# A two-layer diffusion backbone: where the context's low parts stand, and which products carry the modulation sums

## The chip, the cores and the metric

The kernel runs on one core of one Trainium2 chip. The metric is device time in microseconds (us) of one execution, as the median of the runs shown. One execution was recorded by the hardware profiler; its rows give the engines as PE (TensorE's matmuls), PEld (its weight loads), DVE (VectorE), ACT (ScalarE), POOL (GpSimd) and SP (SyncE, which here only issues DMAs). Rows are "start, duration, engine, line, operation, out<-in, shape, count", and in brackets the idle time before the row and what ended it.

## The reference

Two consecutive layers act on 512 latent tokens and 256 context tokens of width 1024. A conditioning vector per kind of token (c for the latents, c_ctx for the context) gives six modulation vectors per layer. Layer 0 mixes tokens with latent attention and neighbourhood attention, layer 1 with a sliding window; each then has a SwiGLU network (width 2816). Cut to what matters here:

```python
for l in range(DEPTH):                       # 2 layers
    sh_a, sc_a, g_a, sh_f, sc_f, g_f = split(silu(c) @ mod_w[l] + mod_b[l], 6)
    csh_a, csc_a, ...                = split(silu(c_ctx) @ mod_w[l] + mod_b[l], 6)
    a_lat = rms_norm(h_lat) * (1 + sc_a) + sh_a
    a_ctx = rms_norm(h_ctx) * (1 + csc_a) + csh_a
    o_lat, o_ctx = mixer(a_lat, a_ctx, ...)          # both kinds use the same weights
    h_lat = h_lat + g_a * o_lat
    h_lat = h_lat + g_f * swiglu(modulate(h_lat, sh_f, sc_f), w_gate_up[l], w_down[l])
    if l == 0: the same for h_ctx with the context's vectors
return rms_norm(h_lat, final_norm)
```

All is float32, and the kernel keeps that accuracy.

## The kernel before

**Products.** TensorE multiplies a rounded format (fp32r) here. Every float32 operand is split into a high part (the rounded value, ACT) and a low part (the rest, DVE), and a product is three matmuls: high by high, high by low, low by high. Splits of weights read L335 (ACT, high) and L336 (DVE, low), and in the pairs below L1377 and L1378. Tokens lie in the columns: 0 to 511 latents, 512 to 767 context; 1024 features are eight tiles of 128 rows.

**Start.** `modulate` (L426) makes the modulated tile k in three steps: a scaled tile (DVE, L433), its high part (ACT, L434) and its low part (DVE, L435). `latent(k)` does so for the 512 latent columns and `context(k)` for the 256 context columns, each followed by products of the kind of L767 to L769 (`three`), which add over k into six PSUM banks, t = 0 to 3 for the latents and 4, 5 for the context. When a latent bank is complete, 128x128 blocks of it are copied out (L502 on DVE, L503 on ACT). Behind this comes the input projection (L346 to L349), whose weights are split by L335 and L336, and further modulation sums of layer 0 (L240 on DVE, L257 on POOL, L258 on ACT).

**Network of layer 0.** The 22 tiles of the hidden width are done in six groups: 0 to 3, 4 to 7, 8 to 11, 12 to 15, 16 to 19, and 20, 21; they are called groups 1 to 6 here. A tile is a `Pair`: gate and up products by a scheme of seven products instead of eight, over two halves of the 768 columns (c1 and c2, 384 each). `head`, `body` and `tail` share it out: the tail of a pair comes behind the head of the next, and the tail of a group's last pair comes just ahead of the group's down products. A pair's weights (two of 512 KB, SP) are combined on DVE (L1412, L1413, L1416, L1420) and split (L1377, L1378). Its tail ends with `t + y` (L1447) and, for c2 and then c1, the product silu x up (L1449), its high part on ACT and its low part on DVE (L1378). After each group but the last come eight down products, m = 0 to 7 (`down0`): the 768-column sum so far ("home") is fetched from memory by POOL (L1233 `p<-home`), the product runs over the group's tiles (L346 to L349) into one bank of 512 and one of 256 columns, DVE adds each to the fetched tile (`add_residual`, L1229), and POOL stores it (L1544 `home<-p`).

**Modulation sums of layer 1.** They need 64 weighted sums over 512 KB blocks of `mod_w`: one DVE instruction each (L302, 128x1024, 1.22 us). 48 blocks are fetched by POOL (L292), all into one buffer (tag `rope0`), 16 of them serve two sums. `late_step(place)` takes the next block: its L302 is placed behind the instruction `place` on DVE, and then the fetch of the following block is issued on POOL. LATE says where the steps are taken: its second part gives for each tile j the number of steps in its pair (the first behind the body, one more behind the preceding pair's tail if the number is over 1, one more behind its own head if over 2); its third part gives for each group the down products m after which a step is taken. When the units have run out, further steps do nothing.

**Order of the work.** A scheduler orders the instructions of each engine by simulated times (SCHED); `behind` and `after` add order constraints between instructions, which need no semaphore on one engine. Each engine then runs its list in order, so an instruction that waits holds up all behind it. POOL's DMA issues are in such a list too.

## Time and profile before

| what | value |
|---|---|
| median of 3 runs | 1574.36 us (1573.1 to 1575.22) |
| profiled execution | 1578.6 us, its span 1576.8 us |
| granted TensorE clock, mean | 0.993 |
| busy in the span | PE 97%, DVE 75%, ACT 50%, POOL 18% |
| chain that ended last | PE 77%, DVE 10%, DMA 6%, ACT 3% |
| L302 (sums of layer 1) | 64 of 1221 ns |
| L292 (their fetches) | 48 of 512 KB |

How to read it: since PE is busy for nearly the whole span, a row of another engine matters where a PE row has brackets that name it, and in what it makes late further on. In a row of the waits by group stand the total, the number and the longest of the waits. In a table by stretch the columns are the stretch, its length, the busy time of PE, PEld, DVE, ACT and POOL with their instruction counts, the granted clock (1.00 is full), the DMA share and GB/s.

### The profile page before, as it was taken

How to read it: one execution, taken by the hardware profiler on the slowest of the kernel's cores; microseconds unless marked ns; L12 is line 12 of the kernel's file. 1: busy time of each engine (PE TensorE's matmuls, PEld its weight loads, DVE VectorE, ACT ScalarE, POOL GpSimd, SP SyncE). 2: the span in 40 equal slices, each digit the busy share in tenths (PEclk: the TensorE clock that was granted, in tenths of full speed). 3: DMA queues.
4: the chain of work that ended last, by engine and by line, in shares of the span. 5: the costliest groups of instructions: out<-in, count | busy, mean ns of one | idle time of the engine just before them, and what ended most of it. 6: DMA issues, size and time to landing. Idle time of an engine off the chain costs nothing.

```text
span 1576.8 us, 26525 instructions
## 1 busy us (share of the span) xinstructions
PE 1529.3 (97%) x10016; PEld 1372.7 (87%) x10016; DVE 1174.8 (75%) x2346; ACT 796.1 (50%) x1607; POOL 276.3 (18%) x302
## 2 busy tenths in 40 slices
PE   6999999999999999999999999999999999999998
PEld 4787778887998999999998988877889999899998
DVE  3885777685878587686858676879976778678685
ACT  4563677775465243242423335558856545354453
POOL 0144724320111101102111132470012000000001
PEclk9999999999999999999999999999999999999999
DMA  9645242004654444647466485110225133323322
GB/s 318 249 131 174 79 127 76 11 7 160 207 168 144 151 167 162 219 126 272 157 198 229 144 325 185 54 41 2 69 76 164 54 97 125 99 89 128 84 97 88
DMA packets 76463, 214.90 MB, mean 136 GB/s; under 512 B 9872, under 2 KB 16400, under 8 KB 76336
## 3 DMA queue, kind: packets, MB, share of 16 engines
q1 hardware_dynamic: 59216, 144.42, 28.1%
q0 software_dynamic: 15968, 67.24, 12.3%
q8 instruction: 78, 1.28, 0.3%
q10 hardware_dynamic: 1152, 1.57, 0.3%
q14 instruction: 49, 0.40, 0.1%
HBM read 186.97 MB, written 23.07 MB: 133 GB/s over the span
## 4 chain that ended last, share of the span: by engine, by line
PE 77%; DVE 10%; DMA 6%; ACT 3%; issue 2%; POOL 0%; SPq 0%; DVEq 0%; ACTq 0%; POOLq 0%
PE pso L557 5%; PE pss L1392 5%; PE pss L1391 5%; PE pss L1390 4%; PE psd L346 4%; PE psd L349 4%; PE psd L348 4%; PE pss L346 4%; PE pss L349 4%; PE pss L348 3%; PE pst L1392 3%; PE pst L1390 3%; PE pst L1391 3%; PE pst L346 3%; PE pst L348 3%; PE pst L349 3%
## 5 line engine op out<-in xcount | busy, mean ns | idle before, releaser
L335 ACT CAST wh<-wr 128x1024 fp32r<-128x1024 f32 (+2 forms) x148 | 115.5, 795 | 208.2 <-DMA wr<-in_w_dn_dram 48.9
L336 DVE TENSOR_TENSOR wl<-wr,wh 128x1024 fp32r<-128x1024 f32 (+2 forms) x145 | 133.0, 924 | 81.1 <-ACT wh L335 79.5
L563 ACT ACTIVATE p<-p,sm 128x512 f32<-128x512 f32 (+3 forms) x144 | 104.9, 729 | 28.5 <-DVE sm L567 26.7
L1390 PE MATMUL pss<-b,wh 128*128 128x384 f32 (+1 forms) x346 | 108.0, 313 | 0.6 <-ACT b L372 0.6
L1391 PE MATMUL pss<-b,wh 128*128 128x384 f32 (+1 forms) x346 | 108.2, 313 | 0.1
L1392 PE MATMUL pss<-b,wl 128*128 128x384 f32 (+1 forms) x346 | 107.3, 312 | 0.0
L348 PE MATMUL psd<-b,wh 128*128 128x512 f32 (+3 forms) x262 | 89.6, 342 | 0.0
L302 DVE CUSTOM_DVE_ANT_0 p<-rope,cond 128x1024 bf16<-128x1024 f32 x64 | 76.9, 1221 | 11.3 <-DMA rope<-in_mod_w_dram 11.2
L292 POOL DMA_DIRECT2D rope<-in_mod_w_dram x48 | 25.7, 535 | 321.1 <-DVE mod L302 308.7
L346 PE MATMUL psd<-b,wh 128*128 128x512 f32 (+3 forms) x222 | 80.0, 361 | 0.9 <-ACT b L476 0.6
L557 PE MATMUL pso<-ph,b 128*64 128x256 f32 (+1 forms) x384 | 78.9, 365 | 0.4 <-DVE ph L502 0.4
L349 PE MATMUL psd<-b,wl 128*128 128x512 f32 (+3 forms) x222 | 78.7, 355 | 0.0
L557 PE MATMUL pso<-pl,b 128*64 128x256 f32 (+1 forms) x384 | 78.5, 363 | 0.0
L1390 PE MATMUL pst<-b,wh 128*128 128x384 f32 (+1 forms) x226 | 70.7, 313 | 2.5 <-DVE p L1229 1.9
L1392 PE MATMUL pst<-b,wl 128*128 128x384 f32 (+1 forms) x226 | 70.7, 313 | 1.4 <-DVE wl L1378 1.4
L1391 PE MATMUL pst<-b,wh 128*128 128x384 f32 (+1 forms) x226 | 70.5, 312 | 0.0
L1377 ACT CAST wh<-pl 128x512 fp32r<-128x512 f32 x78 | 44.9, 620 | 50.0 <-PE pss L1391 22.6
L348 PE MATMUL pss<-b,wh 128*128 128x256 f32 (+3 forms) x216 | 69.2, 321 | 0.0
L1377 ACT CAST wh<-wr 128x1024 fp32r<-128x1024 f32 x39 | 41.0, 1051 | 54.5 <-PE pst L1391 14.6
L346 PE MATMUL pss<-st,wh 128*128 128x512 f32 (+2 forms) x198 | 67.1, 339 | 0.3 <-ACT wh L335 0.3
L349 PE MATMUL pss<-st,wl 128*128 128x512 f32 (+2 forms) x198 | 67.2, 339 | 0.1
L1390 PEld LDWEIGHTS pss<-b,wh 128*128 128x128 f32 x346 | 65.9, 191 | 1.1 <-ACT b L372 0.9
(627 smaller groups left out, 5377.6 us busy)
## 6 DMA issues: line engine op xcount, KB each, us to landing
wr<-in_w_gu_dram SPq DMA_DIRECT2D x88, 512.0 KB, 4.1
rope<-in_mod_w_dram POOLq DMA_DIRECT2D x48, 512.0 KB, 3.9
wr<-in_w_dn_dram SPq DMA_DIRECT2D x73, 256.0 KB, 3.0
wr<-in_w_out_dram SPq DMA_DIRECT2D x32, 512.0 KB, 4.0
p<-home POOLq DMA_DIRECT2D x40, 384.0 KB, 5.4
home<-p POOLq DMA_DIRECT2D x40, 384.0 KB, 5.4
wr<-in_w_in_dram SPq DMA_DIRECT2D x21, 512.0 KB, 4.4
nb<-in_nb_dram SPq DMA_DIRECT2D x16, 384.0 KB, 3.2
```

The source lines that it names most:

```text
L302: behind(V.tensor_tensor_reduce(out=T("p", [P, D], mybir.dt.bfloat16), in0=w, in1=cond[:, v, :], op0=ALU.mult, op1=ALU.add, scale=1.0, sca ...
L335: behind(S.copy(h, r), *after[:1])
L336: behind((G if eng else V).tensor_tensor(lo, r, f(h), op=ALU.subtract), *after[1:])
L346: ins = PE.matmul(o, wh[:, k], mh[:, c], start=first and k == 0, stop=False)
L348: PE.matmul(o, wh[:, k], ml[:, c], start=False, stop=False)
L349: PE.matmul(o, wl[:, k], mh[:, c], start=False, stop=last and k == n - 1)
L557: ins = PE.matmul(o[64 * i : 64 * i + 64, c], v(kt), t, start=n == 0, stop=n == len(moving[i]) - 1)
L563: S.activation(p[:, c], p[:, c], AF.Exp, bias=nm, scale=-1.0, accum_out=dn)
L1377: S.copy(h, t)
L1390: PE.matmul(o, wh, xh, start=first and k == 0, stop=False, skip_group_check=not first)
L1391: PE.matmul(o, wh, xl, start=False, stop=False, skip_group_check=not first)
L1392: PE.matmul(o, wl, xh, start=False, stop=k == 3, skip_group_check=not first)
```

## The change

Two edits. The first changes the table LATE: in groups 3, 4 and 5 the down products take two steps (after m = 2 and 5) where they took four (after 0, 2, 4, 6), and the pairs take more: group 3 one more (8 in all), groups 4 and 5 two more each (10 in all, three in each of the last three pairs), and tiles 20 and 21 take the step that is left over (one sum). The second gives `context(k)` an order constraint: the scaled tile k is placed behind the low part of tile k − 2 on DVE. Lines from 873 on stand two lower in the changed file.

```diff
-LATE = ((0, 1, 3, 5, 7), ()), (0,) * 4 + (1, 2, 2, 2, 1, 2, 2, 2, 1, 2, 3, 2, 1, 2, 3, 2, 0, 0), ((2,), (2,)) + ((0, 2, 4, 6),) * 3
+LATE = ((0, 1, 3, 5, 7), ()), (0,) * 4 + (1, 2, 2, 2, 1, 2, 3, 2, 1, 3, 3, 3, 1, 3, 3, 3, 2, 1), ((2,), (2,), (2, 5), (2, 5), (2, 5))
@@
+    lows = []
+
     def context(k):
-        modulate(A[k], X[k], k, r, 0, 0, 1, CTXS)
+        lows.append(modulate(A[k], X[k], k, r, 0, 0, 1, CTXS, after=lows[-2:-1]))
         for t in (4, 5):
             start_products(k, t)
```

No engine gets more work: PE has 9115 rows in either order, DVE 2332, POOL 299. What moves, at three places.

**DVE at the start**, from the first scaled context tile on. Before (p_564, p_574, ... are the scaled tiles of k = 0, 1, ...; b_99, b_101, ... the low parts):

```order
L433 SCALAR_TENSOR_TENSOR p_564<-b_67,mod_44_123,nb_97 128x256
L433 SCALAR_TENSOR_TENSOR p_574<-b_68,mod_44_123,nb_97 128x256
L433 SCALAR_TENSOR_TENSOR p_584<-b_69,mod_44_123,nb_97 128x256
L433 SCALAR_TENSOR_TENSOR p_594<-b_70,mod_44_123,nb_97 128x256
L433 SCALAR_TENSOR_TENSOR p_604<-b_71,mod_44_123,nb_97 128x256
L433 SCALAR_TENSOR_TENSOR p_614<-b_72,mod_44_123,nb_97 128x256
L433 SCALAR_TENSOR_TENSOR p_624<-b_73,mod_44_123,nb_97 128x256
L433 SCALAR_TENSOR_TENSOR p_634<-b_74,mod_44_123,nb_97 128x256
L502 COPY b_648<-pss_114 128x128
L435 SCALAR_TENSOR_TENSOR b_99<-p_564,mod_42_121,b_98 128x256
L502 COPY b_649<-pss_115 128x128
```

And in the changed kernel:

```order
L433 SCALAR_TENSOR_TENSOR p_564<-b_67,mod_44_123,nb_97 128x256
L433 SCALAR_TENSOR_TENSOR p_574<-b_68,mod_44_123,nb_97 128x256
L502 COPY b_648<-pss_114 128x128
L435 SCALAR_TENSOR_TENSOR b_99<-p_564,mod_42_121,b_98 128x256
L433 SCALAR_TENSOR_TENSOR p_584<-b_69,mod_44_123,nb_97 128x256
L502 COPY b_649<-pss_115 128x128
L502 COPY b_648<-pss_116 128x128
L502 COPY b_649<-pss_116 128x128
L435 SCALAR_TENSOR_TENSOR b_101<-p_574,mod_42_121,b_100 128x256
L433 SCALAR_TENSOR_TENSOR p_594<-b_70,mod_44_123,nb_97 128x256
L502 COPY b_650<-pss_114 128x128
L502 COPY b_650<-pss_115 128x128
```

The low part of tile 0 stands behind two scaled tiles instead of eight, and from there scaled tiles and low parts alternate. Further down in the new order the split of the first projection weight (wl_695) stands between the low parts of tiles 2 and 3.

**DVE at the end of group 4's pairs** (the tail of tile 15) and the first residuals of its down products. Before:

```order
L336 TENSOR_TENSOR wl_8420<-wr_8417,wh_8419 128x512
L1449 TENSOR_TENSOR p_8190<-p_8190,p_8191 128x384
L1447 TENSOR_TENSOR p_8191<-pss_8257,p_8191 128x384
L1378 TENSOR_TENSOR b_8157<-p_8190,b_8156 128x384
L1449 TENSOR_TENSOR p_8190<-p_8190,p_8191 128x384
L1378 TENSOR_TENSOR b_8157<-p_8190,b_8156 128x384
L1229 SCALAR_TENSOR_TENSOR p_8340<-pst_8343,mod_1111_5169,p_8340 128x256
L302 ISA p_8372,mod_1682_8371<-rope_1675_8300,cond_66 128x1024
L302 ISA mod_1682_8371 128x1
L1229 SCALAR_TENSOR_TENSOR p_8340<-psd_8342,mod_1110_5168,p_8340 128x512
```

And in the changed kernel (L1451, L1449, L1380 and L1231 are L1449, L1447, L1378 and L1229 of before):

```order
L336 TENSOR_TENSOR wl_8420<-wr_8417,wh_8419 128x512
L1451 TENSOR_TENSOR p_8190<-p_8190,p_8191 128x384
L302 ISA p_8303,mod_1676_8302<-rope_1674_8260,cond_66 128x1024
L302 ISA mod_1676_8302 128x1
L1449 TENSOR_TENSOR p_8191<-pss_8262,p_8191 128x384
L1380 TENSOR_TENSOR b_8157<-p_8190,b_8156 128x384
L1451 TENSOR_TENSOR p_8190<-p_8190,p_8191 128x384
L1380 TENSOR_TENSOR b_8157<-p_8190,b_8156 128x384
L1231 SCALAR_TENSOR_TENSOR p_8345<-pst_8348,mod_1111_5169,p_8345 128x256
L1231 SCALAR_TENSOR_TENSOR p_8376<-psd_8379,mod_1111_5169,p_8376 128x256
L1231 SCALAR_TENSOR_TENSOR p_8413<-pst_8416,mod_1111_5169,p_8413 128x256
L1231 SCALAR_TENSOR_TENSOR p_8345<-psd_8347,mod_1110_5168,p_8345 128x512
```

A sum now stands between the first L1449 and L1447 of the tail; the one behind the first residual is gone, and the 256-wide parts of residuals 0, 1 and 2 come ahead of the 512-wide ones. At the end of group 5 the rows move in the same way.

**POOL in group 4's down products**, from the load of residual 1 on (home_4258 to home_4265 are the tiles m = 0 to 7). Before:

```order
L1233 DMA p_8376<-home_4259 128x768
L1233 DMA p_8413<-home_4260 128x768
L292 DMA rope_1684_8374<-in_mod_w_dram 128x1024
L1544 DMA home_4258<-p_8340 128x768
L1544 DMA home_4259<-p_8376 128x768
L1233 DMA p_8454<-home_4261 128x768
L1233 DMA p_8491<-home_4262 128x768
L1544 DMA home_4260<-p_8413 128x768
L292 DMA rope_1698_8452<-in_mod_w_dram 128x1024
L1544 DMA home_4261<-p_8454 128x768
L1544 DMA home_4262<-p_8491 128x768
```

And in the changed kernel:

```order
L1235 DMA p_8376<-home_4259 128x768
L1235 DMA p_8413<-home_4260 128x768
L292 DMA rope_1678_8305<-in_mod_w_dram 128x1024
L1546 DMA home_4258<-p_8345 128x768
L1235 DMA p_8454<-home_4261 128x768
L1235 DMA p_8491<-home_4262 128x768
L1235 DMA p_8528<-home_4263 128x768
L1546 DMA home_4259<-p_8376 128x768
L1546 DMA home_4260<-p_8413 128x768
L292 DMA rope_1698_8452<-in_mod_w_dram 128x1024
L1546 DMA home_4261<-p_8454 128x768
L1546 DMA home_4262<-p_8491 128x768
```

The loads of tiles 3, 4 and 5 come directly behind the store of tile 0, where tiles 3 and 4 came behind the store of tile 1 and tile 5 much later.

## The prediction

> **What bounds the kernel now.** I read the page's first part, then the waits of TensorE, then timelines at the places where the change acts.
>
> ```profile
> PE 1529.3 (97%) x10016; PEld 1372.7 (87%) x10016; DVE 1174.8 (75%) x2346; ACT 796.1 (50%) x1607; POOL 276.3 (18%) x302
> ...
> PE pst L810 <- DVE p L387: 12.5, 1, 12.5
> ...
> PE psd L769 <- DVE b L435: 1.2, 1, 1.2
> ```
>
> TensorE works for 1529.3 of 1576.8 us, so all other engines together cost 47.5 us, 12.5 of it one wait at the start that the change doesn't touch. No matmul is removed or added. Only two things can move the time: TensorE's waits, and the speed at which it is clocked. The short wait above, of 1.2, lies at the first place that the diff edits; those at the second are quoted there. I don't gain from DVE's 75%: its work is the same before and after, and only its order counts.
>
> **Part 1, the context's low parts.** The rows are of DVE and TensorE just after the start's latent products.
>
> ```profile
> 53.67 3.26 DVE L433 SCALAR_TENSOR_TENSOR p<-b,mod,nb 128x256 f32<-128x256 f32 x8 [2.48 <-ACT nb L820]
> 56.84 0.29 DVE L502 COPY b<-pss 128x128 f32<-128x128 f32 x1
> 57.04 0.48 DVE L435 SCALAR_TENSOR_TENSOR b<-p,mod,b 128x256 fp32r<-128x256 f32 x1
> ...
> 54.19 0.51 ACT L434 ACTIVATE b<-p,mod 128x256 fp32r<-128x256 f32 x1 [0.55 <-DVE p L433]
> ...
> 56.02 0.39 PE L768 MATMUL psd<-wh,b 128*128 128x512 f32 x1
> ...
> 57.57 0.50 PE L769 MATMUL psd<-wh,b 128*128 128x512 f32 x1 [1.16 <-DVE b L435]
> ...
> 62.32 1.23 DVE L336 TENSOR_TENSOR wl<-wr,wh 128x1024 fp32r<-128x1024 f32 x1 [0.43 <-ACT wh L335]
> ...
> L211 PE MATMUL psd<-ph,cond_col x8: 379/379/403, 116.1 to 116.8; 128*32 128x256 f32 x8
> ```
>
> Before, eight scaled tiles run in a row (3.26 / 8 = 0.41 each), so the first low part comes at 57.04, though its high part is there at 54.19 + 0.51 = 54.70. L769 needs it and waits 1.16. After, two scaled tiles, one copy and low 0: 53.67 + 2 x 0.41 = 54.49, copy to 54.85 (its bank is filled by then, since ACT's copy of a neighbour ran in the same time), low 0 done by 55.3. L769 would start 0.23 behind 56.02, at 56.25. **The wait of 1.16 goes.** Next in line, by the same prices: low 1 needs scaled 2, three copies (0.2 each) and itself, so it is ready at 56.8 against a need at 57.6; low 2 at 58.2 against 59.0. Then the new order lets DVE split the first projection weight (L336, 1.23 long) ahead of low 3: done by 60.2. TensorE covers this with 20-odd products of that projection, which now stand between context tiles 2 and 3 and need the split at about 60.9. If that cover went, the price is at most 1.2 (one L336 before low 3). So part 1 is **−1.2**, bounds −1.2 and +1.2. The background sums of layer 0, which stand behind it on DVE and ACT, begin about 3 us later, because ACT's table load now follows the last high part; the buffers that they hold (ph, pl) are next needed by the products at 116.1 (the last row), and 50 us of TensorE's own projection work lie between, which cover it: nothing, at most 3 if they don't.
>
> **Part 2, fewer sums in the down products.** In group 4 (tiles 12 to 15) TensorE lost most:
>
> ```profile
> 842.53 0.34 PE L1392 MATMUL pss<-b,wl 128*128 128x384 f32 x1
> ...
> 844.74 0.41 PE L1390 MATMUL pst<-b,wh 128*128 128x384 f32 x1 [1.87 <-DVE p L1229]
> ...
> 838.43 0.44 PE L1390 MATMUL psd<-b,wh 128*128 128x384 f32 x1 [0.69 <-DVE p L1229]
> ...
> 828.16 0.75 DVE L1229 SCALAR_TENSOR_TENSOR p<-pss,mod,p 128x512 f32<-128x512 f32 x1 [3.80 <-DMA p<-home]
> ...
> 841.43 0.69 DVE L1412 TENSOR_TENSOR pl<-wr 128x512 f32<-128x512 f32 x1 [2.07 <-DMA wr<-in_w_gu_dram]
> ...
> 843.85 0.75 DVE L1229 SCALAR_TENSOR_TENSOR p<-pst,mod,p 128x512 f32<-128x512 f32 x1
> ...
> 819.77 0.56 POOL L1544 DMA_DIRECT2D home<-p  x1 [4.29 <-DVE mod L302]
> 820.32 1.08 POOL L1233 DMA_DIRECT2D p<-home  x2
> ```
>
> Read from below: POOL issues in order, and what ended the 4.29 us in which it issued nothing was a sum (L302). Only then does it send for the residual tiles 3 and 4 (820.32). They are late, DVE's L1229 waits 3.80 for one, and everything behind it on DVE slips: the next pair's preparation (L1412) gets in front of residual 6, waits 2.07 for its own weights, and TensorE waits 1.87 for that residual's bank. In the new order the loads of residual tiles 3, 4 and 5 follow the store of residual 0 at once, about 4.8 us earlier (POOL was free for them at 819.77 − 4.29 = 815.48 and sent at 820.32), no sum stands between the first three residuals, and both remaining residuals, 6 and 7, precede the second pair's L1412. I take **0.69 + 1.87 = 2.56 off**. The transfers of this stage crowd each other:
>
> ```profile
> 756.00:813.00 57.00, 57.00 (x333) 55.75 (x332) 40.86 (x72) 21.69 (x42) 6.40 (x12) 1.00 0.47 151
> ...
> 813.00:843.00 30.00, 29.18 (x164) 25.79 (x162) 20.22 (x34) 8.38 (x14) 7.01 (x13) 1.00 0.83 288
> ...
> rope<-in_mod_w_dram POOLq DMA_DIRECT2D x8, 512.0 KB, 3.8
> ...
> rope<-in_mod_w_dram POOLq DMA_DIRECT2D x3, 512.0 KB, 7.2
> ...
> wr<-in_w_gu_dram SPq DMA_DIRECT2D x5, 512.0 KB, 7.3
> ```
>
> (First the pairs, then the down products: DMA share 0.47 and 0.83; a sum's 512 KB lands in 3.8 and in 7.2 us.) Two fewer 512 KB fetches there help the rest too, which I don't count.
>
> The stall has a second price, the clock. After 844.74 the matmuls are spaced wider:
>
> ```profile
> 840.00:860.00 20.00, 18.13 (x96) 17.81 (x95) 15.75 (x27) 7.00 (x13) 2.71 (x5) 0.91 0.52 190
> ...
> 845.34 0.34 PE L1391 MATMUL pss<-b,wh 128*128 128x384 f32 x1
> ...
> 848.98 0.34 PE L1392 MATMUL pss<-b,wl 128*128 128x384 f32 x1
> ...
> 851.93 0.33 PE L1392 MATMUL pss<-b,wl 128*128 128x384 f32 x1
> ...
> 213.48 0.63 PE L511 MATMUL psd<-ident_r,p 128*128 128x128 f32 x4 [1.54 <-DVE b L977]
> ```
>
> The window's granted clock is 0.91. From 845.34 to 848.98 lie 12 steps of one matmul in 3.64 us; at the usual 0.174 (848.98 to 851.93 is 17 steps) they would take 2.08. That is 1.56 lost, and it goes with the stall: **−1.56**. A stall of 1.54 at 213.48 is followed by wider spacing as well, those of 0.7 to 1.2 shown here are not.
>
> [...]
>
> Group 5 (tiles 16 to 19) has the same sums, and a smaller stall:
>
> ```profile
> 939.47 1.22 DVE L302 CUSTOM_DVE_ANT_0 p<-rope,cond 128x1024 bf16<-128x1024 f32 x1
> ...
> 940.61 1.22 DVE L1378 TENSOR_TENSOR wl<-wr,wh 128x1024 fp32r<-128x1024 f32 x1
> ...
> 941.88 0.45 PE L1392 MATMUL pst<-b,wl 128*128 128x384 f32 x1 [0.83 <-DVE wl L1378]
> ```
>
> The L302 at 939.47 (1.22) stands just ahead of the split that TensorE waits for. It moves to the pairs: **−0.83**, bounds −0.83 and 0. Group 3 showed no such wait; nothing there.
>
> **What the pairs pay.** Groups 4 and 5 now have three sums in each of their last three pairs. There is one buffer for the sums' weights: a sum, the issue behind it, the landing, the next sum.
>
> ```profile
> 798.42 1.23 DVE L302 CUSTOM_DVE_ANT_0 p<-rope,cond 128x1024 bf16<-128x1024 f32 x1 [0.65 <-DMA rope<-in_mod_w_dram]
> ...
> 799.95 0.53 POOL L292 DMA_DIRECT2D rope<-in_mod_w_dram  x1 [4.84 <-DVE mod L302]
> ...
> 804.26 1.22 DVE L302 CUSTOM_DVE_ANT_0 p<-rope,cond 128x1024 bf16<-128x1024 f32 x1 [1.26 <-DMA rope<-in_mod_w_dram]
> ...
> 807.50 0.55 DVE L1449 TENSOR_TENSOR p<-p,p 128x384 f32<-128x384 f32 x1
> ...
> 809.43 0.55 DVE L1449 TENSOR_TENSOR p<-p,p 128x384 f32<-128x384 f32 x1
> ...
> 810.56 0.56 DVE L1378 TENSOR_TENSOR b<-p,b 128x384 fp32r<-128x384 f32 x1 [0.58 <-ACT b L1377]
> ...
> 811.68 0.28 PE L346 MATMUL pst<-b,wh 128*128 128x256 f32 x1
> ...
> 813.22 0.40 PE L348 MATMUL psd<-b,wh 128*128 128x512 f32 x1
> ```
>
> Both L302 waited for data, so their distance, 804.26 − 798.42 = 5.84 us, is the cycle; the third sum of the last pair can start at 804.26 + 5.84 = 810.1 and ends at 811.3. In the new order it stands between the first L1449 (807.50) and L1447, and DVE can do nothing else meanwhile. Behind it: L1447, the low part of the first half (done near 812.4, where TensorE wants it at about 811.7), L1449, ACT's high part (the wait of 0.58 before 810.56) and the low part of the second half, near 813.9 to 814.1, where the 512-wide products first want it at about 813.2 (L348 multiplies by the low part). So TensorE waits about **0.9 in group 4 and 0.9 in group 5**. Bounds for each: 0 if the sums shift earlier (the cycle without waits is nearer 5.3), and 2.5, two L302 of 1.22 with no margin left. I take 0.9, since the cycle was measured at the same spot. The pairs before have no such tail: their products are followed by the next pair's, which hide 1.22 us of DVE at 75% load. The one sum that ends up in group 6 stands between two products of running pairs: nothing, at most its own 1.22.
>
> **The sum** against the profiled execution (1578.6, span 1576.8, and 1.8 around it): −1.2 − 2.56 − 1.56 − 0.83 + 1.8 = −4.3. The profiled run is 4.2 over the median of the three runs, 1574.36; the difference carried over gives **1570.1**.
>
> **Rivals.**
> A. *The crowd stays.* The weights of the next pair (7.3 to land) delay L1412, not the sums; POOL's earlier loads then only move the crowd forward. For it: the 2.07 was ended by a weight DMA. Against: residuals 6 and 7 now stand ahead of that wait. The group 4 and 5 gains (4.95) fail and the tails cost: 1574.36 − 1.2 + 1.8 = **1575.0**. Chance 0.22.
> B. *The one buffer becomes the bound* (slower). The last fetch of groups 4 and 5 now travels with the loads of residuals 0 to 2 and the first down weights. At the crowded landing of 7.2 instead of 804.26 − 799.95 = 4.31 the third sum starts 2.9 later, TensorE waits 0.9 + 2.9 = 3.8 twice, and both stalls are past 1.54, so the clock drops: 2 x (3.8 + 1.56) = 10.7. 1574.36 − 1.2 − 4.95 + 10.7 = **1578.9**. It decides from waits of about 3 us each, where the gains are eaten. Against: the share before 813 is 0.47. Chance 0.14.
> C. *Part 1 does not pay*: the split of the projection weight takes the place of the wait it removes. 1570.1 + 1.2 = **1571.3**. Chance 0.10.
> D. *The clock drop isn't the stall's* and comes all the same, whatever the waits: 1570.1 + 1.56 = **1571.7**. Against: both drops shown began behind a stall of 1.5 or more. Chance 0.06. [...]
>
> **How the numbers follow.** Forecast 0.48, rivals 0.22, 0.14, 0.10, 0.06. About 0.2% (3.1 us) is what a measurement of this kernel can tell from no change: 1571.2 to 1577.5. The forecast is faster, C straddles the edge (0.02 faster, 0.08 same), A and D are same, B slower: 0.50, 0.36, 0.14. The low end leaves out the tails' cost and takes a little of the run spread: 1570.1 − 1.8 − 0.8 = 1567.5; the high end is A with the same: 1575.8. Forecast alone: 1567.5 to 1572.
>
> **What would show it.** Right: no wait at the first L769; no L1390 of group 4 waiting on L1229, a granted clock of 1.00 there; POOL's loads of residuals 3 to 5 right behind the store of residual 0; waits under 1.5 us on L1449's low parts at the end of groups 4 and 5. Wrong: idle TensorE of 3 us or more at those two tails with L302 waiting for its weights in front (B), or L1229 still late behind L1412 (A).

## The result, and the profile after

| what | before | after |
|---|---|---|
| median of 22 runs each, us | 1575.23 (1573.08 to 1579.12) | 1580.36 (1574.77 to 1585.33) |
| ratio, with its 95% interval | 1 | 1.0029 [1.0020, 1.0037] |
| profiled execution, its span, us | 1578.6, 1576.8 | 1581.22, 1579.5 |

The change makes the kernel slower, by 0.0029 x 1575.23 = 4.6 us. The forecast was 1570.1 and faster; the range ended at 1575.8. First the engines' busy times of the changed kernel, then TensorE's waits by group (total, number, longest); only the rows that are new are shown.

```profile
PE 1529.7 (97%) x10016; PEld 1371.3 (87%) x10016; DVE 1175.2 (74%) x2346; ACT 797.6 (50%) x1607; POOL 274.3 (17%) x302
```

```profile
PE psd L767 <- DVE b L502: 2.6, 1, 2.6
PE psd L1392 <- ACT wh L1379: 1.8, 1, 1.8
...
PE psd L346 <- DVE st L744: 1.0, 1, 1.0
...
PE pst L346 <- DVE st L744: 0.8, 1, 0.8
```

No engine works more than before. The group that part 1 of the prediction aimed at (L769 waiting on L435, 1.2) and those of part 2 (L1390 waiting on L1229) are gone. Four others stand in their place: two at the first input projection (L346 on L744), one between groups 5 and 6 (L1392 on L1379), and one of 2.6 in layer 0's value projection.

**Where the profiled execution is ahead or behind.** The table takes the start of the same-numbered matmul of TensorE in both traces (the changed one minus the other).

| place (time in before) | after minus before, us |
|---|---|
| ahead of the context's products, 50 | −0.5 |
| behind the context's products, 82 | −2.0 |
| behind the first projection, 117 | +0.3 |
| 211, behind a clock drop of before alone (183.4) | −2.2 |
| 270 | +0.2 |
| within group 4's down products, 820 | +1.7 |
| end of group 4, 863 | −1.6 |
| late in group 5's down products, 933 | −1.3 |
| group 6, 973 | +1.0 |
| 1008 | +2.1 |
| end | +2.6 |

Both edits win where they were meant to win (−1.5 from 50 to 82, and −3.3 from 820 to 863) and lose it again a little later. The loss of 2.4 between 211 and 270 is the value projection's wait with a clock drop (2.3 and some 1.6, less a drop of before's at 214), and is not put down to the change: none of the experiments' profiles has this wait, and what goes with it is told in the section on the hardware.

**Part 1, after.** The timeline: start, duration, engine, line, operation, and in brackets the wait.

```profile
70.50 0.39 PE L769 MATMUL psd<-st,b 128*128 128x512 f32 x1
70.54 0.88 DVE L502 COPY b<-psd 128x128 f32<-128x128 f32 x4 [1.05 <-ACT b L503]
...
105.28 0.69 DVE L744 TENSOR_TENSOR st<-psd,st 64x512 fp32r<-64x512 f32 x1
106.12 0.36 PE L346 MATMUL psd<-b,wh 128*128 128x256 f32 x1 [0.98 <-DVE st L744]
...
110.02 0.50 PE L346 MATMUL pst<-b,wh 128*128 128x512 f32 x1 [0.80 <-DVE st L744]
```

And the context's last product and the same copies in the timeline of before:

```profile
67.91 0.39 PE L769 MATMUL psd<-st,b 128*128 128x512 f32 x1
67.95 0.88 DVE L502 COPY b<-psd 128x128 f32<-128x128 f32 x4 [1.05 <-ACT b L503]
```

The copies of the context's two banks, and layer 0's background sums behind them, come 2.6 us later (70.54 against 67.95; the first sum on POOL at 72.95 against 70.36). TensorE's new order has 20-odd projection products between context products, so those banks are complete later (last product at 70.50 against 67.91). The eviction L744 stands in DVE's list among these sums, and TensorE wants its bank at 106: 0.98 + 0.80 lost.

**Group 4, after.**

```profile
813.03 0.39 PE L348 MATMUL pst<-b,wh 128*128 128x256 f32 x1 [0.19 <-DVE b L1380]
...
817.11 0.54 POOL L1546 DMA_DIRECT2D home<-p  x1 [4.24 <-DVE p L1231]
820.12 1.60 POOL L1235 DMA_DIRECT2D p<-home  x3 [2.47 <-issue]
...
824.84 0.75 DVE L1231 SCALAR_TENSOR_TENSOR p<-pss,mod,p 128x512 f32<-128x512 f32 x1 [3.77 <-DMA p<-home]
...
834.07 0.69 DVE L1414 TENSOR_TENSOR pl<-wr 128x512 f32<-128x512 f32 x1 [3.37 <-DMA wr<-in_w_gu_dram]
...
847.42 0.44 PE L1394 MATMUL pst<-b,wl 128*128 128x384 f32 x1 [0.82 <-DVE wl L1380]
```

POOL sends for residuals 3 to 5 at 820.12 (residuals 3 and 4 at 820.32 before), so DVE still waits 3.77 for one. What went is a step after it: residual 5 now stands ahead of the first pair's L1414, which waits 3.37 for its weights, and residuals 6 and 7 ahead of the second pair's (843.88), which waits for nothing. TensorE has one wait of 0.82 left, for a split (L1380).

**Between groups 5 and 6, after.** SP's and POOL's issues, and those who wait:

```profile
931.27 2.12 POOL L1235 DMA_DIRECT2D b<-home  x4
...
931.69 0.39 SPq L136 DMA_DIRECT2D wr<-in_w_dn_dram  x1
...
943.29 0.83 ACT L1379 CAST nb<-wr 128x768 fp32r<-128x768 f32 x1 [5.49 <-DMA wr<-in_w_dn_dram]
944.03 1.13 ACT L1379 CAST wh<-ph 128x512 fp32r<-128x512 f32 x2
...
945.22 0.45 PE L1392 MATMUL psd<-st,wh 128*128 128x384 f32 x1 [1.85 <-ACT wh L1379]
```

The same in before:

```profile
930.04 0.39 SPq L136 DMA_DIRECT2D wr<-in_w_dn_dram  x1
...
931.98 2.12 POOL L1233 DMA_DIRECT2D b<-home  x4
...
934.29 0.84 ACT L1377 CAST nb<-wr 128x768 fp32r<-128x768 f32 x1 [0.39 <-DMA wr<-in_w_dn_dram]
```

The transfer is the down weights of the last group (384 KB). Before, SP issued it 1.9 us ahead of POOL's burst of four "home" tiles (384 KB each, which group 6 adds to); after, 0.4 us behind the burst's start. Its row in the DMA view of each, ending with the time from issue to landing, and then that of after:

```profile
wr<-in_w_dn_dram SPq DMA_DIRECT2D x1, 384.0 KB, 4.2
```

```profile
wr<-in_w_dn_dram SPq DMA_DIRECT2D x1, 384.0 KB, 11.6
```

Nobody needs those weights before group 6's down products. But their split stands on ACT and DVE ahead of tile 21's split (`wh<-ph`), which TensorE wants now: ACT waits 5.49, TensorE 1.85.

### The profile page after: what moved, and what is told of

Its sections match the earlier page's. It is cut to its first block, busy times and chain, and to the rows that moved or that the text cites. A ratio compares the mean times of both kernels' runs of the same rounds, so it can differ in the third digit from the quotient of the medians.

```text
span 1579.5 us, 26510 instructions
## 1 busy us (share of the span) xinstructions
PE 1529.7 (97%) x10016; PEld 1371.3 (87%) x10016; DVE 1175.2 (74%) x2346; ACT 797.6 (50%) x1607; POOL 274.3 (17%) x302
## 4 chain that ended last, share of the span: by engine, by line
PE 36%; DVE 6%; DMA 4%; issue 2%; ACT 1%; POOL 1%; DVEq 0%; ACTq 0%; POOLq 0%
PE pss L1394 2%; PE pss L1392 2%; PE pss L1393 2%; PE pso L557 2%; PE pst L1394 2%; PE pst L1392 2%; PE pst L1393 2%; PE psd L346 1%; DMA wr<-in_w_gu_dram 1%; PE psd L348 1%; PE psd L349 1%; PE pss L346 1%; PE pss L349 1%; PE pss L348 1%; DMA wr<-in_w_dn_dram 1%
## 5 line engine op out<-in xcount | busy, mean ns | idle before, releaser
L335 ACT CAST wh<-wr 128x1024 fp32r<-128x1024 f32 (+2 forms) x148 | 115.4, 795 | 214.1 <-DMA wr<-in_w_dn_dram 46.1
L336 DVE TENSOR_TENSOR wl<-wr,wh 128x1024 fp32r<-128x1024 f32 (+2 forms) x145 | 134.2, 932 | 75.4 <-ACT wh L335 71.5
L1392 PE MATMUL pss<-b,wh 128*128 128x384 f32 (+1 forms) x346 | 107.7, 312 | 0.6 <-ACT b L372 0.6
L346 PE MATMUL psd<-b,wh 128*128 128x512 f32 (+3 forms) x222 | 80.3, 362 | 2.0 <-DVE st L744 1.0
L1392 PE MATMUL pst<-b,wh 128*128 128x384 f32 (+1 forms) x226 | 70.5, 312 | 0.0
L1379 ACT CAST wh<-wr 128x1024 fp32r<-128x1024 f32 x39 | 41.0, 1052 | 52.7 <-PE pst L1393 14.7
L346 PE MATMUL pss<-st,wh 128*128 128x512 f32 (+2 forms) x198 | 67.4, 340 | 0.3 <-ACT wh L335 0.3
L1379 ACT CAST wh<-pl 128x512 fp32r<-128x512 f32 x78 | 45.0, 619 | 44.6 <-PE pss L1393 22.1
L1392 PEld LDWEIGHTS pss<-b,wh 128*128 128x128 f32 x346 | 65.6, 190 | 1.1 <-ACT b L372 0.9
```

The costliest lines, as they stand in the source:

```text
L335: behind(S.copy(h, r), *after[:1])
L336: behind((G if eng else V).tensor_tensor(lo, r, f(h), op=ALU.subtract), *after[1:])
L346: ins = PE.matmul(o, wh[:, k], mh[:, c], start=first and k == 0, stop=False)
L1379: S.copy(h, t)
L1392: PE.matmul(o, wh, xh, start=first and k == 0, stop=False, skip_group_check=not first)
```

## The experiments

Theory: group 5's row is the loss, by a late transfer whose split blocks ACT; group 4's third sum and part 1 each give their gain back. Rivals: POOL's earlier residual loads crowd the weights (rival A of the forecast), the one buffer of the sums decides (rival B), or the loss is in part 1 alone. Each ratio is to the kernel before on the same chip; a plain value without a sign is a ratio, with its 95% interval.

### The two edits apart

Part 1 alone (the `lows` edit without the table), and the table alone.

> Part 1 alone (the context's low parts between its scaled tiles; the table of sums as before). Theory A, from the two profiles: the wait of 1.2 at 57 goes, but two new waits of 1.0 and 0.8 come at 106 and 110, where the evictions of the first projection stand in DVE's list behind a modulation chain that began 2.6 us later: together +0.6 to +1, that is between no change and +2 against the kernel before. Theory B, the forecast: -1.2, with nothing behind it.

> Part 2 alone (the table of sums of the changed kernel, the start as before). By the profiles: group 3's and 4's ends +0.5 and +0.9, group 4's down products -3.3, group 5's end and what follows +4: +2 in all. The forecast was -3.1. If instead part 1 is the whole loss, this is at or below -2.

Part 1: 1575.07 us, 1.0004 [0.9988, 1.0020]. The table: 1580.17, **1.0046** [1.0028, 1.0065]. The table is the loss, and a larger one than its stages in the profiles had added up to (+2 expected, 0.0046 x 1574.42 = 7.2 us measured); part 1 is worth nothing that can be seen. Part 1's profile has both new waits (0.98 at 107.17, 0.78 at 111.06).

### One group's row at a time

```diff
 before     (1, 2, 2, 2, 1, 2, 2, 2, 1, 2, 3, 2, 1, 2, 3, 2, 0, 0), ((2,), (2,)) + ((0, 2, 4, 6),) * 3
+g4_only    (1, 2, 2, 2, 1, 2, 2, 2, 1, 3, 3, 3, 1, 2, 3, 2, 0, 0), (..., (0, 2, 4, 6), (2, 5), (0, 2, 4, 6))
+g5_only    (1, 2, 2, 2, 1, 2, 2, 2, 1, 2, 3, 2, 1, 3, 3, 3, 0, 0), (..., (0, 2, 4, 6), (0, 2, 4, 6), (2, 5))
+g3_only    (1, 2, 2, 2, 1, 2, 3, 2, 1, 2, 3, 2, 1, 2, 3, 2, 2, 1), (..., (2, 5), (0, 2, 4, 6), (0, 2, 4, 6))
```

> The table changed in group 4 alone (two sums taken from its down products, three in each of its last three pairs). Theory A: the stall of 1.9 and the half clock behind it go, the tail costs under 1: -2 to -4. Rival: the third sum of the last pair costs as much as the stall did: 0 or slower.

> The table changed in group 5 alone. Theory A: the down weights of the last group arrive late in a fuller queue, a cast of them stops ACT for over 5 us, and TensorE waits 1.9 and loses clock later: +2 to +4. Rival (the tail's third sum alone costs, and the stall of 0.8 goes): between -0.8 and +0.9.

> The table changed in group 3 alone (one sum more in its pairs, two fewer in its down products, one left over for group 6). By the profile of the changed kernel: nothing to +0.5 us, ratio 1.000.

Group 4: 1578.11, **1.0021** [1.0007, 1.0034]. Group 5: 1579.74, **1.0038** [1.0023, 1.0053]. Group 3: 1574.13, 0.9989 [0.9975, 1.0004]. The three together (0.0048) make up the table's 0.0046. Group 4's row was expected to gain 2 to 4 us; it lost 3.3, so the rival held, that its third sum takes the gain back, and more. The timeline of group 4's row alone:

```profile
809.96 1.23 DVE L302 CUSTOM_DVE_ANT_0 p<-rope,cond 128x1024 bf16<-128x1024 f32 x1 [2.33 <-DMA rope<-in_mod_w_dram]
...
812.18 0.39 PE L348 MATMUL pst<-b,wh 128*128 128x256 f32 x1 [0.65 <-DVE b L1378]
...
825.81 0.75 DVE L1229 SCALAR_TENSOR_TENSOR p<-pss,mod,p 128x512 f32<-128x512 f32 x1 [5.42 <-DMA p<-home]
...
826.87 0.68 DVE L336 TENSOR_TENSOR wl<-wr,wh 128x512 fp32r<-128x512 f32 x1
827.58 0.33 SPq L136 DMA_DIRECT2D wr<-in_w_gu_dram  x1
...
834.65 0.69 DVE L1412 TENSOR_TENSOR pl<-wr 128x512 f32<-128x512 f32 x1 [3.58 <-DMA wr<-in_w_gu_dram]
...
848.00 0.44 PE L1392 MATMUL pst<-b,wl 128*128 128x384 f32 x1 [1.93 <-DVE wl L1378]
```

And in before, the split of down weights that frees the buffer, and the issues of the next pair's two weights (the second at 821.56):

```profile
820.84 0.69 DVE L336 TENSOR_TENSOR wl<-wr,wh 128x512 fp32r<-128x512 f32 x1 [1.12 <-ACT wh L335]
...
817.51 4.37 SPq L136 DMA_DIRECT2D wr<-in_w_gu_dram  x2
```

The third sum starts at 809.96 where 810.1 was forecast, and its direct price is 0.65. Then comes what wasn't counted. The next pair's weights are two transfers, and SP sends for each when a split L336 has freed its buffer. The first is sent for 2.9 us later (820.42 against 817.51), the second, for which L1412 waits, 6.0 later (827.58 against 821.56): its L336 now stands behind residual 3's L1229, and DVE waits 5.42 there for the load that POOL sent for at 819.55. Before, that L336 (820.84) stands ahead of this wait. L1412 waits 3.58, and TensorE 1.93.

### Group 4: the loads or the tail?

First, group 4's row with POOL's loads of residuals 3, 4, 5 held back behind the stores of residuals 1, 1 and 3, about where they stood before. Second, two sums instead of three in the last pair (the spare one goes to tile 20).

```diff
-        t = fetched(m, slice(0, NT))
+        t = B(tag="p")
+        behind(G.dma_start(t, home[m]), *([stores[(1, 1, 3)[m - 3]]] if ci == 3 and 2 < m < 6 else ()))
```

```diff
-(..., 1, 3, 3, 3, 1, 2, 3, 2, 0, 0)
+(..., 1, 3, 3, 2, 1, 2, 3, 2, 1, 0)
```

> The same in group 4: the table changed there alone, and POOL's loads of residuals 3 to 5 held as before the change. Theory A (the crowd of early loads): from 1.002 to 1.000 or below. Rival (the third sum in the pairs' tail costs it): it stays at 1.002.

> Group 4's table changed, but with two sums, not three, in its last pair (one sum is left over for group 6). Theory A: the third sum of the last pair keeps DVE waiting for its weights, the splits of the down weights come 2 us late, SP's next weights 3 us late, and the next group's first pair waits 2 us for them and loses clock; without it the ratio falls from 1.002 to 1.000 or below. Rival: three loads of residuals in front of the down weights do it, which this kernel keeps: it stays at 1.002.

Loads held: 1578.08, 1.0017 [1.0000, 1.0034], with a wait of 2.35 at 844.40. Two sums in the tail: 1573.54, **0.9987** [0.9972, 1.0003], and TensorE has no wait in group 4's down products and the next pair. The intervals of three sums (from 1.0007) and of two (to 1.0003) don't touch, so this row restores the time, and holding the loads does not. But the two-sum kernel differs by more than the sum. The scheduler moved its loads of residuals 3 to 5 as well:

```profile
802.63 0.54 POOL L1233 DMA_DIRECT2D p<-home  x1
805.54 1.07 POOL L1233 DMA_DIRECT2D p<-home  x2 [2.38 <-issue]
```

They are sent for ahead of the first residual's add (808.00), where the row alone sends at 819.55, 5.9 us behind it (813.65), and DVE no longer waits for them. So whether the third sum costs by its own time, or by making these loads late, isn't told apart: a kernel with three sums and early loads was not run. Loads that come too early are not the loss; loads that come too late may be.

### Group 5: the loads, the split, or the burst?

All three start from group 5's row alone. First, residual loads 3 to 5 held as above (`ci == 4`). Second, the split of the last group's down weights held behind tile 21's splits on ACT and DVE; no DMA is touched. Third, POOL's burst of "home" tiles held behind the last store; no other engine's order changes.

```diff
+    def parts(t, h, lo, after=(), held=()):
+        high = behind(S.copy(h, t), *(x for x, _ in held))
+        marks["low"] = behind(V.tensor_tensor(lo, t, f(h), op=ALU.subtract), *after, *(x for _, x in held))
...
-            parts(r[:, c], *(x[:, c] for x in t))
+            parts(r[:, c], *(x[:, c] for x in t), held=held if a == 0 else ())
```

```diff
-        G.dma_start(t[:, c], home[m][:, c])
+        behind(G.dma_start(t[:, c], home[m][:, c]), *(stored[-1:] if tag == "b" else ()))
```

> Group 5's table changed, and POOL's loads of residuals 3, 4 and 5 held behind the stores of residuals 1, 1 and 3, as before the change. Theory A: the early loads crowd the pair's weights and with them the last group's down weights; then those land in 4 to 6 us and the ratio falls from 1.004 to 1.001 or less. Rival: the loads' place doesn't matter (the third sum's place, or the fuller ends of the pairs, do): it stays near 1.004.

> Group 5's table changed, and the split of the last group's down weights (high part on ACT, low part on DVE) held behind the splits of tile 21's weights on both engines. Theory A: those weights land late (11.6 us), and a cast that waits for them stops ACT and DVE in front of the splits that TensorE needs; then the wait of 1.9 to 2.5 goes and the ratio falls from 1.004 to about 1.001. Rival: the queue as a whole is late; the wait only moves to the next weights or to the last down products, and the ratio stays near 1.004.

> Group 5's table changed, and the loads of the last group's residuals (POOL, eight of 384 KB) held behind the last store of group 5; the order of ACT, DVE and TensorE is that of group 5's kernel alone. Theory A: those loads stand in front of the last group's down weights, which land in 12 us; then they land in 4 to 7, the wait of 2.5 goes and the ratio falls from 1.004 to about 1.001. Rival: they are late for the pair's own weights or the stores: landing stays over 10 us, 1.004.

Loads held: 1577.44, 1.0014 [0.9998, 1.0029], but its profile keeps the wait (2.26 at 939.82): inconclusive, since the stall that it was to remove is there although the ratio fell. Split held: 1576.13, 1.0013 [0.9997, 1.0028]. Burst held: 1576.88, 1.0010 [0.9995, 1.0025]. Neither of the last two has a TensorE wait between groups 5 and 6. Group 5's row alone, for comparison:

```profile
937.12 0.83 ACT L1377 CAST nb<-wr 128x768 fp32r<-128x768 f32 x1 [6.35 <-DMA wr<-in_w_dn_dram]
...
939.04 0.69 PE L1390 MATMUL psd<-st,wh 128*128 128x384 f32 x1 [2.48 <-ACT wh L1377]
```

And the DMA row of the transfer with the burst held (its cast then runs at 932.50 without a wait):

```profile
wr<-in_w_dn_dram SPq DMA_DIRECT2D x1, 384.0 KB, 4.9
```

With the split held TensorE doesn't wait, though the transfer is as late as ever where its landing was read (11.8 us, in all_casts_held below); with the burst held it lands in 4.9 us, against 12.4 in the row alone. Both ends of the chain are shown in the traces: the burst makes it late, and the split's place makes lateness a stall. The medians say less: all three edits lie at 1.0010 to 1.0014, the one that keeps the stall among them, and their intervals overlap that of the row alone (from 1.0023) by up to 0.0006. That this one stall is the whole 0.0038 is not shown.

### Part 1: the products held

Part 1, with the first projection's products held behind context's last product, so that TensorE's order is that of before:

```diff
-                mm3([(o, c)], (w[0][:, k : k + 1], w[1][:, k : k + 1]), A[k : k + 1], k == 0, k == KT - 1)
+                ins = mm3([(o, c)], (w[0][:, k : k + 1], w[1][:, k : k + 1]), A[k : k + 1], k == 0, k == KT - 1)
+                if k == 0:
+                    behind(ins, *ended)
```

> Part 1 with the first projection's products held behind the context's last product, so that TensorE's order is that of before. Theory A: the copies of the last two banks and the modulation chain behind them on DVE are no longer 2.6 us late, the waits at 106 and 110 go, and the gain of about 1.2 at 57 stays or shrinks by small waits for the later low parts: 0 to -1.2 against before. Rival (the chain is late for another reason, the table load behind the last high part): the waits at 106 and 110 stay, +0.6 to +1.

1574.05, 0.9995 [0.9982, 1.0008]. The waits at L769 and both at L744 are gone, so the reorder of TensorE's list had made them. Yet the time stays: its profile has a wait for a fetch a little later,

```profile
126.86 0.62 PE L211 MATMUL pst<-ph,cond_col 128*32 128x256 f32 x4 [1.95 <-DMA ph<-in_mod_wp_dram]
```

which before has with 1.21 (at 125.89), after with 0.30, and part 1 alone not at all. TensorE gets there earlier and waits there longer: 0.74 of the gain of 1.16 goes back there in this execution, and a clock drop at 128.8, which before doesn't have, takes the rest.

### The whole change, mended

```diff
 mended              part 1 held, split held, and two sums in the last pairs of groups 4 and 5
 all_home_held       the whole change, burst held
 all_casts_held      the whole change, split held, and the first weight split of layer 1 held too:
-            after=(marks["middle"],) * (m > 3)
+            after=(marks["middle"],) * (m > 2)
 all_home_win_held   the whole change, burst held, and that weight split held
 all_but_g5          the whole change, group 5's row as before
 held_and_g4_tail2   part 1 held, and of the table only group 4 with two sums in its last pair
 held_and_g3         part 1 held, and of the table only group 3
```

> Both parts with the three causes taken out: the first projection's products behind the context's, two sums in the last pairs of groups 4 and 5, the split of the last group's down weights behind tile 21's. Theory A: what is left are the gains: 1.2 at the start, 1 to 1.7 of group 4's usual waits, 0.8 of group 5's: -2 to -3.5 against before. Rival (the gains are taken back by waits on DMAs later on): within 1 us of before.

> The whole change, with nothing but POOL's loads of the last group's residuals held behind the last store of group 5 (all other engines' orders as in the changed kernel). Theory A: the late down weights of the last group are most of the loss: from 1.003 to 1.000 or 0.999, no wait on ACT's casts near 945. Rival: the tails of groups 4 and 5 and the start share the loss: it stays at 1.002 or above.

> The whole change with two splits moved back in the lists of ACT and DVE, no transfer touched: that of the last group's down weights behind tile 21's splits, that of layer 1's first projection weight behind tile 21's body. Theory A (late weights stop ACT and DVE at the passage from group 5 to group 6): the waits of 1.9 and 2.3 there are gone and the ratio falls from 1.003 to 1.001 or less. Rival (the loss is in the tails of groups 4 and 5, at the start, or spread): 1.002 to 1.003.

> The whole change with the last group's residual loads held, as before, and now the split of layer 1's first projection weight behind tile 21's body too. Theory A: holding the loads only handed the lateness to that weight, which stopped ACT from 948 to 951; with both, the wait of 2.3 at 955 goes and the ratio falls from 1.003 to 1.001 or less. Rival: as above, 1.002 to 1.003.

> The whole change with group 5's row of the table as before. Theory A (group 5's part is the loss): 1.000. Rival (group 4's tail or the start cost it): 1.002 or above.

> What did not lose, together: part 1 with the projection's products held (0.9995), and group 4's table with two sums in its last pair (0.9987). If the parts add: 0.998, -3 us. Rival: the gain at the start is taken back at the waits on DMAs behind it (1.2 at 126): 0.999.

> Part 1 with the projection's products held and the table changed in group 3 alone: if the parts add (0.9995 and 0.9989), 0.998; the same rival.

| kernel | us | ratio, 95% |
|---|---|---|
| mended | 1577.28 | 1.0015 [0.9998, 1.0032] |
| all_home_held | 1578.51 | 1.0033 [1.0018, 1.0048] |
| all_casts_held | 1574.79 | **1.0006** [0.9994, 1.0018] |
| all_home_win_held | 1574.05 | 1.0013 [0.9993, 1.0032] |
| all_but_g5 | 1575.88 | **1.0008** [0.9995, 1.0021] |
| held_and_g4_tail2 | 1573.11 | 1.0001 [0.9986, 1.0017] |
| held_and_g3 | 1573.07 | 0.9996 [0.9982, 1.0010] |

The burst held in the whole change was a miss: it removes the wait at 945 and the time stays at 1.0033. Its timeline shows why:

```profile
950.98 1.05 ACT L335 CAST wh<-wr 128x1024 fp32r<-128x1024 f32 x1 [2.56 <-DMA wr<-in_w_in_dram]
...
955.47 0.45 PE L1394 MATMUL pst<-st,wh 128*128 128x384 f32 x1 [2.33 <-ACT p L1441]
```

The lateness went to the next transfer, layer 1's first projection weight, whose split stands on ACT ahead of tile 21's copy L1441. With both splits held (all_casts_held, no transfer touched) a wait of 0.57 is left there (0.62 in before), and the whole change comes out level with before, though it still has part 1's two waits. Its interval (to 1.0018) lies below that of the change (from 1.0020). Group 5's row put back does about the same (1.0008). The burst held together with that second split has no longer wait there either (0.57), but its runs spread to 1583.58 and its interval tells nothing (0.9993 to 1.0032). "Mended", of which −2 to −3.5 was expected, was a miss: it held only the first of the two splits and put more sums into group 6; its profile has waits of 1.86 at 951.83 and 1.51 at 964.05 there.

No version is shown to beat before. The lowest ratios, group 4 with two sums in its tail (0.9987) and group 3's row (0.9989), both hold 1 in their intervals, and with part 1 held, where 0.998 was expected if the parts add, they are at 1.0001 and 0.9996.

## Why the prediction was wrong

**Part 1 (−1.2): the wait went as worked out, the step "cost at nothing" failed.** L769's 1.16 is gone, and DVE's order did what was said. The prediction saw that the background sums would start some 3 us later (2.6 measured), though not for the reason that it gave: with the products held, ACT's table load is as late as in the changed kernel (63.36; 62.81 after, 57.72 before), and DVE's first sum is early again (70.25; 72.02 after, 69.44 before). It named TensorE's 50 us of projection work as cover until the products at 116.1. It looked for the sums' own consumer, and not for what stands between the sums in DVE's list: the eviction L744, wanted at 106. Price 0.98 + 0.80. Rival C had part 1 come to nothing, by another wait than the one that did it.

**Group 4 (−0.69 − 1.87): the cause was read rightly; the loads' new time and the size were wrong.** POOL's loads didn't move up by 4.8 us but by 0.2. The third sum stands ahead of residual 0's adds, so its store went out at 817.11 (814.93 before), and POOL lost 2.47 more at the issue. DVE still waited 3.77 at residual 3. That such a wait is what makes the stall, as the prediction had it, the traces bear out. In five of the 20 kept executions DVE does not wait for residual 3's load (the two-sum row of group 4 and group 3's row, each with and without part 1 held, and "mended"), and TensorE has no wait over 0.15 in group 4's down products. In the other 15 DVE waits 2.3 to 5.7 there, and TensorE 0.6 to 2.6 in all but one. Why group 3's row, with group 4's as before, has these loads in time was not followed up. That the order of residuals 5 to 7 before L1414 took the 2.56 down to 0.82 is argued from the order alone. And the term was sized from one execution. In kernels whose groups 3 and 4 are as before, the place shows 1.04 (part 1), 0.70 + 0.88 (group 5's row), 0.49 + 1.12 (part 1 held), and 1.4 to 1.7 in the three variants of group 5's row:

```profile
843.65 0.41 PE L1392 MATMUL pst<-b,wh 128*128 128x384 f32 x1 [1.04 <-DVE p L1231]
```

So about 1.0 to 1.7 was to be had, not 2.56.

**The clock (−1.56): mis-sized.** None of those six executions has a clock drop there. The drop came with the longer stall of the one profiled execution of before; group 4's row alone has one too (at 849.0, behind its 1.93), and the changed kernel has none behind its 1.85 at 945. What the traces show of it stands below.

**The tails (+0.9 each): right in place and in time, wrong in reach.** The third sum came at 809.96 (810.1 forecast) and TensorE's wait behind it was 0.65 in group 4's row alone and 0.19 after. What the step left out is everything that comes later with it: residual 0's adds and its store, the loads of residuals 3 to 5 behind that store, the L336 that stands behind residual 3, a buffer, SP's queue, the next pair's weights (3.58 on DVE, 1.93 on TensorE). Three sums against two in the tail is 1.0021 against 0.9987, some 5 us, where 0.9 was priced; the two-sum kernel's early loads are part of that difference.

**Group 5 (−0.83): wrong sign.** The sum ahead of L1378 did move. But the last group's down weights fell behind POOL's burst, and the price was 1.85 at TensorE after, 2.48 alone, and by the medians of that row 0.0038 x 1574.42 = 6 us. "The one sum that ends up in group 6: nothing" looked at that sum and not at the transfers beside it.

**The rivals.** Rival A had the right kind of cause (crowding moves on and a weight is late) at another place and transfer; it would have given 1575.0, and the time was 1580.36 on medians that stand at 1575.23 for before. Rival B had the sign and nearly the time (1578.9), and its cause fell: TensorE's waits at the two tails were 0.19 to 0.65, not 3.8. Rival D, that the drop isn't the stall's, has support in part: see below.

**What stays open.** In several kernels the profiled execution was among the fastest of its runs: the table alone 1574.65, its lowest, with a median of 1580.17; group 5's row 1573.61, lowest too, with 1579.74. So the traces show where time is lost, and which edit restores it is shown by medians, but what the longer runs do in addition has not been seen. The parts don't add up either: group 4's row costs 0.0021 alone, and the whole change without group 5's row, which has it, only 0.0008 [−0.0005, +0.0021]; the intervals overlap, and no run settles it.

## What to carry to other kernels

A stall of 1 to 2 us in one profiled execution is a sample: look for it in other executions before its size, and above all the clock drop behind it, goes into a sum. When work moves from one stage to another, follow the queues that it passes (whose transfer is now behind which burst, which buffer comes free later), and ask of each late arrival what stands behind its first user on that engine. Between groups 5 and 6 of the whole change the cure for a late transfer wasn't an earlier transfer, which only passed the lateness on, but a later split: an instruction that nobody needs yet must not stand ahead of one that is needed, on an engine that runs in order.

## What the runs showed of the hardware that was not expected

**Beside POOL's burst, SP's queue moves a third of the bytes with as many packets.** The DMA queues of after from 931.5 to 943.3, the life of the late transfer (q0 is POOL's, q1 SP's; packets, MB, share of the 16 engines' time), and those of before from 930 to 934.3:

```profile
q0 software_dynamic: 632, 2.93, 70.9%
q1 hardware_dynamic: 673, 1.05, 24.6%
```

```profile
q1 hardware_dynamic: 544, 0.92, 59.4%
q0 software_dynamic: 76, 0.31, 21.5%
```

After, the queues move about as many packets (632 and 673), but POOL's are 4.6 KB each (2.93 / 632) and SP's 1.6 KB (1.05 / 673). Before, SP moved 0.92 MB in 4.3 us; after, 1.05 MB in 11.8. The issue moved by 2.4 us against the burst (1.94 ahead of it, 0.42 behind its start), and the landing takes 11.6 instead of 4.2. Why the two counts come out about even there, no run tells.

**The clock drop does not follow from the stall's length alone.** The same wait of 1.54 stands near 211 in all 20 kept executions (213.48 in before); a drop begins behind it in 12 of them. The stretch 205 to 220 (length, busy times, granted clock, DMA share, GB/s), first of before, then of held_and_g4_tail2:

```profile
205.00:220.00 15.00, 12.93 (x86) 9.64 (x87) 12.19 (x31) 13.80 (x33) 4.63 (x5) 0.89 0.45 133
```

```profile
205.00:220.00 15.00, 12.07 (x87) 9.62 (x85) 13.01 (x31) 13.04 (x32) 5.74 (x6) 1.00 0.42 133
```

The same wait, 0.89 in one and 1.00 in the other. The clock records of the traces show each drop as one stretch of 3.41 us at half speed: at 22.9, 183.4, 214.1, 845.6 and 1057.2 in before, at 22.2, 240.6, 981.3 and 1059.8 after, and a longer one (6.25 and 6.22) at the end of each. Within one execution they start whole multiples of 3.413 us apart (in before 47, 9, 185 and 62 of them), so the idle time is looked at here in windows of that length, counted from the drops. The wait of 1.87 in before lies in one window; the wait of 1.85 at 945 in after is cut by an edge at 943.78, and only the first has a drop behind it. The two windows, first of before, then of after (TensorE's busy time is the number behind the length):

```profile
842.15:845.56 3.41, 1.54 (x10) 1.22 (x9) 3.41 (x7) 1.28 (x2) 0.28 (x1) 1.00 0.10 42
```

```profile
943.78:947.19 3.41, 1.97 (x11) 1.90 (x12) 3.03 (x5) 2.80 (x6) 0.75 (x2) 1.00 1.05 387
```

Between the first 25 us and the last 10, all 13 windows of the 20 executions in which TensorE was busy for less than half were followed by a drop (before has one of them, with 1.54 busy at 842.15, and after one, with 0.79 at 237.22). Of those between half and 70% only some were (in before the one with 2.36 at 179.96 was, the one with 2.27 at 190.20 was not), so the share alone does not decide. The drop at 981.3 comes behind no wait at all, but behind 24 matmuls of one column:

```profile
978.56 2.73 PE L398 MATMUL psd<-ones,p 128*128 128x1 f32 x24
```

In before, the longest wait in the 7 us ahead of 183.4 is 0.85 (at 181.78).

None of the waits shown here ahead of a drop (0.85 to 2.6) is as long as one such window. What sets a drop off is not shown.

**A small cast on VectorE took three to five times as long beside GpSimd.** Two casts of 32x768 in after, GpSimd's work beside them, and who waits:

```profile
234.35 1.81 POOL L1123 TENSOR_TENSOR st<-b,st 64x768 fp32r<-64x768 f32 x1 [6.25 <-ACT st L1122]
234.69 5.31 DVE L1119 CAST st<-b 32x768 fp32r<-32x768 f32 x2
...
240.51 0.49 PE L767 MATMUL psd<-wh,b 128*128 128x256 f32 x1 [2.62 <-DVE b L502]
```

In before the same pair takes 2.98 (as in the table alone), and TensorE waits 0.28 there:

```profile
238.38 2.98 DVE L1117 CAST st<-b 32x768 fp32r<-32x768 f32 x2
```

That is 2.66 and 1.49 for one cast. Without GpSimd beside it (idle from 219.85 to 223.91) one such cast takes 0.55, in after:

```profile
223.21 0.55 DVE L1119 CAST st<-b 32x768 fp32r<-32x768 f32 x1
```

No run here tells GpSimd's work from another cause; it stands beside the pair in before as well (L1121, 1.80 from 238.05). The 5.31 appeared in after's profiled execution alone; the other 19 have 2.98, those with the same edits among them. So 2.6 − 0.28 = 2.3 us of that profile, and the drop at 240.6 behind it, are put down to chance and not to the change.
